# Where four one-and-two-column tiles lie in SBUF: one shared tile of 512 bytes in a two-layer transformer trunk

## The chip, the cores and the metric

The kernel runs on one core of a Trainium2 chip. The metric is the device time of one execution in microseconds (us). The profile is one execution, recorded by the hardware profiler; its span runs from the first to the last instruction.

## The reference

The kernel computes a two-layer encoder trunk on one sequence of 512 tokens and 1024 features, in float32:

```python
for i in range(DEPTH):                                   # DEPTH = 2
    h = _rmsnorm(x, norm_mix[i])
    if i % 2 == 0:                                       # layer 0
        q, k, v, u = split(h @ ab_w_in)
        a_out = diff_attention(q, k, v, ...)             # 4 heads, p1 - lambda * p2
        b_out = pool_mixer(u, pool_w, pool_scale)        # trailing means over 2, 4, 8, 16 tokens
        x = x + concat([a_out, b_out]) @ ab_w_out
    else:                                                # layer 1
        x = x + gla_mixer(h, w_in, w_gk_up, ...)         # gated linear attention, 4 heads
    h = _rmsnorm(x, norm_ffn[i])
    x = x + square(relu(h @ ffn_w1[i])) @ ffn_w2[i]      # 1024 -> 4096 -> 1024
return _rmsnorm(x, norm_final)
```

Here lambda is one number, `exp(sum(l0 * l1)) - exp(sum(l2 * l3)) + 0.2`, made of four small vectors of the input.

## The kernel before

Everything is kept transposed: features on the 128 partitions, 512 tokens along the free axis. A weight array is streamed from HBM in units of 1 MB (`load`, L92), and each half unit, 128 x 1024 float32, is split by ScalarE (`wh`, L103) and VectorE (`wl`, L104) into two parts in the type float32r. Activations are split in the same way, into a high and a low part. A product then takes three passes of TensorE (`mm3`, L123 to L127): `wh` with the high part, `wh` with the low part, `wl` with the high part. The weights are the stationary operand, a slice of 128 columns, which is 512 bytes of each partition; the activation row of 512 tokens, 2048 bytes of each partition, is the moving operand. `proj_T` (L129) makes one result of 128 features by 512 tokens from eight such triples, so 24 passes in a row, and each pass loads its own weights (LDWEIGHTS, engine PEld) while the pass before it runs.

Two kinds of rows are the moving operand of `mm3`:

- `ah` and `al` (L120): the split inputs of a block. They are read by the projections, by the output projection (`add_out`, L399) and by the first product of each feed-forward block (`ffn`, L419).
- `hi` and `lo` of L423, taken from the buffers `r16`: the split squares of the hidden layer. They are read by the second product of a feed-forward block (`ffn`, L433; `last_chunk`, L459). The profile prints every tile of `row8` and `row16` as `r`.

`ffn` handles the 4096 hidden features in four chunks of 1024. For each it makes eight rows with the first array (8 x 24 = 192 passes with `ah` and `al`), then eight results with the second array (192 passes with `r`). The two kinds of stages alternate without a pause. The last chunk of the last block is done by halves of the tokens (`last_chunk`), in 2 x 192 passes of 256 columns; each half ends in its part of the final norm and the stores of its outputs.

The gate of layer 1 has 16 passes in which the roles are mixed (L522): the moving operand is `ah` or `al`, the stationary one a tile of `row8`.

**Where tiles lie.** All tiles come from one pool. The pool gives each tag its buffers one behind the other, in the order in which the tags are first used, and rounds each tile up to a multiple of 32 bytes. Of the built program's places in a partition, in bytes:

| tag | before: start | modulo 512 | after: start | modulo 512 |
|---|---|---|---|---|
| `par`, `x`, `wraw`, `ones`, `onesr` | 16512 and on | 128 | same | 128 |
| `wh`, `wl` (4 + 4 buffers of 4096) | 51328 and on | 128 | same | 128 |
| `ah`, `al` (12 + 12 of 2048) | 84096 and on | 128 | same | 128 |
| `nacc`, `tmp`, `rb` | 133248 and on | 128 | same | 128 |
| the four small columns | 149632, 149664, 149696, 149728 | 128, 160, 192, 224 | 149632 (one tile) | 128 |
| `row8`, `row16` (8 + 16 of 2048) | 149760 and on | 256 | 150144 and on | 128 |
| `small` (24 of 32) | 198912 and on | all multiples of 32 | 199296 and on | all multiples of 32 |
| `tmp2` (6 of 2048) | 199680 and on | 0 | 200064 and on | 384 |
| `u`, `lvl`, `rb2`, `state` | 212000 and on | | all 384 bytes further | |

A buffer of `row8`, `row16`, `ah` or `al` has 2048 bytes and a slice of weights 512, so within each of these rows of the table every buffer or slice starts at the same place modulo 512.

The four small columns are the sums (L269), their exponentials (L271), minus lambda (L273) and the scaled gain (L276). A handful of instructions of a few hundred ns at most touch them, all in layer 0.

The order of the instructions on each engine is the scheduler's, and is fixed when the program is built.

Of the kernel before, what the change touches and what calls it, by code (L numbers as in the profile page):

```python
# [27 lines left out]

# columns of the packed parameter array
C_MIX0, C_FFN0, C_MIX1, C_FFN1, C_FIN = 0, 8, 16, 24, 32  # L30
# [5 lines left out]
def trunk(ctx: ExitStack, tc: tile.TileContext, xT, par, lvl, lam4, wqk0, wu0, wv0, poolw, wo0,  # L36
# [10 lines left out]

    # buffers by how long they are held: a row of 8 and a row of 16
    def row8(n=S, dt=F32):
# [17 lines left out]

    # what the tensor engine waits for goes ahead of the rest
    def soon(n=300):
        return tc.high_priority(n)  # L70

    # ---- parameters, inputs and the first unit of weights
    prm = T([P, N_PAR], "par", 1)
# [16 lines left out]

    # ---- weight streaming: raw float32 units, split into two parts of 12 bits
    def load(src):  # L92
# [14 lines left out]
    class Stream:  # L107
        """Halves of the units of one weight array, in order."""

# [19 lines left out]
    def proj_T(w, act, ts=slice(0, S)):  # L129
        """[128 features, tokens] from a half unit [128, 8, 128] and split inputs."""  # L130
        hi, lo = w
        ps = PS("mm", (P, ts.stop - ts.start))
        for kb in range(KB):
            c = slice(kb * P, (kb + 1) * P)
            ah, al = act[kb]
            mm3(ps, (hi[:, c], lo[:, c]), (ah[:, ts], al[:, ts]), kb == 0, kb == KB - 1)
        return ps

    def proj_tok(stream, act):
        """Four [128 tokens, 512 features] results from half units [128, 2, 512]."""  # L140
        pss = [PS("mm") for _ in range(NT)]
        for pair in range(KB // 2):
            wh, wl = stream.next()
            for t in range(NT):
                ts = slice(t * P, (t + 1) * P)
                for j in range(2):
                    kb = 2 * pair + j
                    c = slice(j * S, (j + 1) * S)
                    ah, al = act[kb]
                    PE.matmul(pss[t], ah[:, ts], wh[:, c], start=kb == 0, stop=False)  # L150
                    PE.matmul(pss[t], al[:, ts], wh[:, c], start=False, stop=False)  # L151
                    PE.matmul(pss[t], ah[:, ts], wl[:, c], start=False, stop=kb == KB - 1)  # L152
        return pss

    def split_scaled(src, col):
        """Parts of src * (a value per partition)."""
        ah, al = act_tiles()
        A.activation(ah, src, AF.Copy, scale=col)
        V.scalar_tensor_tensor(out=al, in0=src, scalar=col, in1=ah.bitcast(F32), op0=ALU.mult, op1=ALU.subtract)
        return ah, al  # L160
# [7 lines left out]
    def spread(r):  # L168
        """Values per token [128, n] along the free axis of every partition, in PSUM."""
        n = r.shape[-1]  # L170
        ps = PS("ax", (P, n * P))
        for t in range(n):
            PE.matmul(ps[:, t * P:(t + 1) * P], r[:, t:t + 1].to_broadcast([P, P]), ident, start=True, stop=True)
        return ps

    def col_sums(sq, c):
        """Sums over all partitions, on every partition, of a tile to which c is added."""
        n = sq.shape[-1]
        ps, hi, lo = PS("ax", (P, n)), tmp(n, F32R), tmp(n, F32R)
        A.activation(hi, sq, AF.Copy)  # L180
        V.scalar_tensor_tensor(out=lo, in0=sq, scalar=c, in1=hi.bitcast(F32), op0=ALU.add, op1=ALU.subtract)
        PE.matmul(ps, ones_r, hi, start=True, stop=False)  # L182
        PE.matmul(ps, ones_r, lo, start=False, stop=True)
        return ps
# [7 lines left out]
    def rsqrt(r, v, inv):  # L192
        """(v * inv) ** -0.5: a first value by logarithm, then one Newton step."""
        A.activation(r, v, AF.Ln, scale=inv)
        A.activation(r, r, AF.Exp, scale=-0.5)
        return newton(r, v, inv, tmp(r.shape[-1]))

    def neg_recip(r, v, inv):
        """-1 / (v * inv), in the same way."""
        t = tmp(r.shape[-1])  # L200
# [6 lines left out]
    class Norm:  # L207
        """Sums of squares over the features of x, tile by tile."""

# [24 lines left out]
    def per_token(rb):  # L234
        """One row of rb as [128 tokens, 4]."""
        ps = PS("ax", (P, NT))
# [5 lines left out]

    # ================= layer 0: attention and pooling =================
    act = []
# [17 lines left out]

    # lambda on every partition
    l4 = tmp(256)
# [3 lines left out]
    V.tensor_tensor(lp, l4v[:, :, 0, :], l4v[:, :, 1, :], ALU.mult)  # L268
    ls = T([P, 2], "lsum", 1)  # L269
    V.tensor_reduce(out=ls, in_=lp, op=ALU.add, axis=AX.X)  # L270
    le = T([P, 2], "lexp", 1)  # L271
    A.activation(le, ls, AF.Exp)
    neglam = T([P, 1], "nlam", 1)  # L273
    V.tensor_tensor(neglam, le[:, 1:2], le[:, 0:1], ALU.subtract)
    V.tensor_scalar(out=neglam, in0=neglam, scalar1=-LAM_INIT, scalar2=None, op0=ALU.add)
    sub8 = T([P, 1], "sub8", 1)  # L276
    V.tensor_scalar(out=sub8, in0=prm[:, C_SUB:C_SUB + 1], scalar1=1.0 - LAM_INIT, scalar2=None, op0=ALU.mult)
# [12 lines left out]
    def scores(h, qts):  # L290
        """Score blocks of 128 queries each, masked, in two banks; minus their scaled maxima."""
        banks = [PS("ax"), PS("ax")]
# [18 lines left out]
    def softmax(h, qt, views, neg):  # L311
        """p1 - lambda * p2, transposed, into the head's tiles."""
        n = (qt + 1) * P
# [29 lines left out]
    def attend(h):  # L343
        """The products with the values, normalised."""
        po = PS("ax")
# [26 lines left out]

    # pooling branch
    pw = tmp2().rearrange("p (g c) -> p g c", g=4)
# [24 lines left out]
    def add_out(arr, src, col):  # L399
        """x += (split inputs) @ weights; the next block's inputs and norm."""  # L400
        st = Stream(arr)
# [50 lines left out]
    def last_chunk(s2, a, rb2):  # L452
        """The end of the last block by halves of the tokens, each with its final norm."""
        for half in range(2):
# [34 lines left out]

    # constants of layer 1  # L490
    lv = T([P, NLEV + 1, P], "lvl", 1, U8)
# [10 lines left out]

    # ================= layer 1: gated linear attention =================
    with soon(800):
        smask = row8()
        G.memset(smask, 1.0)
        G.memset(smask.rearrange("p (c t) -> p c t", t=P)[:, :, 0:1], 0.0)
        # gate weights: both parts of the 16 columns side by side, so two passes make all the products;
        # four copies of them, for the stacked product of the up-projection
        gk2 = [row8(dt=F32R).rearrange("p (k a b) -> p k a b", k=4, a=4) for _ in range(2)]  # L510
        for i in range(2):
            src = gkr[:, 4 * i:4 * i + 4, :, :]
            A.activation(gk2[i][:, :, :, 0:16], src, AF.Copy)
            V.tensor_tensor(gk2[i][:, :, :, 16:32], src, gk2[i][:, :, :, 0:16].bitcast(F32), ALU.subtract)
        # rows 0-63: the weights' high part, rows 64-95: the low part
        wu = row8(dt=F32R)
# [7 lines left out]
    rb = nrm.rb()  # L524
    # rows 0-31 and 64-95: the high part of the gate's input, rows 32-63: the low part
    gkf = tmp2()
# [37 lines left out]
    def weights(h):  # L564
        """Products within chunks, and the factors across them, of one head."""
        ps = proj_T(st.next(), act)
# [8 lines left out]
        b3 = b.rearrange("p (c t) -> p c t", t=P)  # L575
        # across chunks
        e = row16()
# [16 lines left out]
        kdt.append(kd)  # L594
        # within chunks: the diagonal, then pairs (second half, first half) of ever smaller blocks
        at = row16()
# [6 lines left out]
        for l in range(NLEV - 1):  # L603
# [12 lines left out]
            if s >= 16:  # L616
                # whole blocks, which start at partitions that a product can be put at
                for p0 in range(0, P, 2 * s):
# [7 lines left out]
            for c in range(NT):  # L626
# [3 lines left out]
                              psl.rearrange("p (c t) -> p c t", t=P))  # L630
        # neighbours, as the diagonal: the products' sums over the features
        d = tmp(S // 2)
# [23 lines left out]
    def outputs(h):  # L656
        """Transposed outputs of one head, normalised: two tiles [128 features, tokens]."""
        half, hh = divmod(h, 2)
# [34 lines left out]

    # the parts of the heads, in the order that keeps every engine supplied
    for h in range(3):
# [28 lines left out]

# ---- layout on the host
def _blocks_T(w):
    """Rows in blocks of 1024, columns in units of 256: [units, 128, 2, 8 * 128]."""
    k, n = w.shape
    w = w.reshape(k // D, KB, P, n // 256, 2, P)
    return np.ascontiguousarray(w.transpose(0, 3, 2, 4, 1, 5)).reshape(-1, P, 2, 1024)  # L730


def _blocks_tok(w):
    """Columns in blocks of 512, rows in units of 512: [units, 128, 2, 2 * 512]."""
    n = w.shape[1]
# [64 lines left out]
```

## Time and profile before

| | |
|---|---|
| time, median of 3 runs | 1136.92 us (1136.45 to 1137.26) |
| span of the profiled execution | 1135.0 us |
| its own time | not listed apart; the runs' median is 1.92 us above its span |
| TensorE (PE) busy | 1118.5 us, 99% of the span |
| weight loads (PEld) | 904.5 us, 80% |
| VectorE (DVE), ScalarE (ACT) busy | 641.5 us (57%), 468.2 us (41%) |
| granted TensorE clock, mean | 0.996 of the full 2.4 GHz |

The profile draws a matmul with a duration of about 0.4 us, since it is pipelined: the next one starts some 0.23 us later. The rate of the passes is therefore read from starts, or from the count of weight loads in a stretch, not from the durations. In the views `r` is a tile of `row8` or `row16`, and `tmp` one of `tmp` or `tmp2`.

### The profile page before, as it was taken

What the parts mean: (1) busy time and instruction counts of PE and PEld (TensorE: products, weight loads), DVE (VectorE), ACT (ScalarE), POOL (GpSimd) and SP (SyncE); (2) the same over time, 40 slices, a digit from 0 to 9 for tenths busy, and PEclk for the clock granted to TensorE, in tenths of its full rate; (3) what the DMA queues carried; (4) which work ended last, traced back from release to release, by engine and by line L of the source; (5) the groups of instructions that cost most, each with busy time, mean ns of one, the idle gap of its engine ahead of it and who ended that gap; (6) DMA issues with size and microseconds to landing.
All of it is one profiled execution on the core that took longest, in us unless ns stands there. A gap on an engine that the chain in (4) does not pass through costs nothing.

```text
span 1135.0 us, 13269 instructions
## 1 busy us (share of the span) xinstructions
PE 1118.5 (99%) x5312; PEld 904.5 (80%) x5312; DVE 641.5 (57%) x1024; ACT 468.2 (41%) x748; POOL 7.2 (1%) x26
## 2 busy tenths in 40 slices
PE   8999999999999999999999999999999999999996
PEld 6676778888888888888777788888888888888896
DVE  7757866423433455456898867555323434455485
ACT  7445544323322422334645466434323313312463
POOL 0000000000000000000000000000000000000001
PEclk9999999999999999999999999999999999999998
DMA  7221233232222323222121312232232323223252
GB/s 247 80 90 38 84 109 111 74 111 79 107 103 84 111 74 111 81 106 92 58 75 38 113 38 74 74 112 88 98 109 77 111 74 112 91 96 107 79 187 75
DMA packets 19229, 107.21 MB, mean 94 GB/s; under 512 B 2048, under 2 KB 5120, under 8 KB 7008
## 3 DMA queue, kind: packets, MB, share of 16 engines
q1 hardware_dynamic: 19024, 106.34, 26.9%
q8 instruction: 42, 0.69, 0.2%
q14 instruction: 19, 0.16, 0.0%
q10 hardware_dynamic: 144, 0.03, 0.0%
HBM read 104.26 MB, written 2.10 MB: 94 GB/s over the span
## 4 chain that ended last, share of the span: by engine, by line
PE 92%; DVE 2%; issue 2%; ACT 2%; DMA 1%; SPq 0%; POOL 0%; POOLq 0%; DVEq 0%; ACTq 0%
PE psmm L127 26%; PE psmm L126 26%; PE psmm L125 26%; PE psmm L150 2%; PE psmm L152 2%; PE psmm L151 2%; PE psax L301 1%; PE psax L628 1%; PE psax L621 1%; PE psax L347 1%; DMA wraw<-in_wqk 1%; PE psax L182 1%; PE psax L678 0%; PE psax L663 0%; PE psax L329 0%
## 5 line engine op out<-in xcount | busy, mean ns | idle before, releaser
L103 ACT ACTIVATE wh<-wraw 128x1024 fp32r<-128x1024 f32 x190 | 200.9, 1059 | 517.6 <-PE psmm L126 480.1
L104 DVE TENSOR_TENSOR wl<-wraw,wh 128x1024 fp32r<-128x1024 f32 x190 | 232.2, 1223 | 264.3 <-ACT wh L103 263.6
L125 PE MATMUL psmm<-ah,wh 128*128 128x512 f32 x864 | 339.6, 393 | 4.9 <-ACT wh L250 4.9
L126 PE MATMUL psmm<-al,wh 128*128 128x512 f32 x864 | 339.4, 393 | 0.0
L127 PE MATMUL psmm<-ah,wl 128*128 128x512 f32 x864 | 338.9, 392 | 0.0
L126 PE MATMUL psmm<-r,wh 128*128 128x512 f32 (+1 forms) x576 | 213.0, 370 | 0.1
L125 PE MATMUL psmm<-r,wh 128*128 128x512 f32 (+1 forms) x576 | 213.1, 370 | 0.0
L127 PE MATMUL psmm<-r,wl 128*128 128x512 f32 (+1 forms) x576 | 213.0, 370 | 0.0
L125 PEld LDWEIGHTS psmm<-ah,wh 128*128 128x128 f32 x864 | 162.7, 188 | 41.1 <-ACT wh L250 5.6
L126 PEld LDWEIGHTS psmm<-al,wh 128*128 128x128 f32 x864 | 162.7, 188 | 36.5 <-issue 2.1
L127 PEld LDWEIGHTS psmm<-ah,wl 128*128 128x128 f32 x864 | 162.8, 188 | 35.7 <-issue 1.6
L126 PEld LDWEIGHTS psmm<-r,wh 128*128 128x128 f32 x576 | 108.2, 188 | 20.7 <-DVE r L428 0.3
L127 PEld LDWEIGHTS psmm<-r,wl 128*128 128x128 f32 x576 | 108.2, 188 | 20.4
L125 PEld LDWEIGHTS psmm<-r,wh 128*128 128x128 f32 x576 | 108.1, 188 | 20.4
L439 DVE TENSOR_TENSOR r<-r,psmm 128x512 f32<-128x512 f32 x32 | 22.0, 687 | 88.7 <-PE psmm L127 88.7
L428 DVE TENSOR_TENSOR r<-tmp,r 128x512 fp32r<-128x512 f32 x64 | 44.3, 692 | 6.5
L427 DVE TENSOR_TENSOR tmp<-tmp 128x512 f32<-128x512 f32 x64 | 43.8, 684 | 0.0
L426 ACT ACTIVATE r<-tmp 128x512 fp32r<-128x512 f32 x64 | 40.5, 634 | 2.0
L150 PE MATMUL psmm<-wh,ah 128*128 128x512 f32 x96 | 39.1, 407 | 0.0
L151 PE MATMUL psmm<-wh,al 128*128 128x512 f32 x96 | 38.5, 401 | 0.0
L152 PE MATMUL psmm<-wl,ah 128*128 128x512 f32 x96 | 38.2, 398 | 0.0
L425 ACT ACTIVATE tmp<-psmm 128x512 f32<-128x512 f32 x64 | 36.9, 577 | 0.0
(183 smaller groups left out, 813.0 us busy)
## 6 DMA issues: line engine op xcount, KB each, us to landing
wraw<-in_w2b SPq DMA_DIRECT2D x20, 1024.0 KB, 4.8
wraw<-in_w1a SPq DMA_DIRECT2D x16, 1024.0 KB, 4.8
wraw<-in_w2a SPq DMA_DIRECT2D x16, 1024.0 KB, 4.8
wraw<-in_w1b SPq DMA_DIRECT2D x16, 1024.0 KB, 4.8
wraw<-in_wo SPq DMA_DIRECT2D x8, 1024.0 KB, 4.7
wraw<-in_wqk SPq DMA_DIRECT2D x7, 1024.0 KB, 4.9
wraw<-in_wv SPq DMA_DIRECT2D x6, 1024.0 KB, 4.7
wraw<-in_wg SPq DMA_DIRECT2D x4, 1024.0 KB, 4.9
```

The costliest lines, as they stand in the source:

```text
L103: A.activation(hi, src, AF.Copy)
L104: V.tensor_tensor(lo, src, hi.bitcast(F32), ALU.subtract)
L125: PE.matmul(ps, wh, ah, start=first, stop=False)
L126: PE.matmul(ps, wh, al, start=False, stop=False)
L127: PE.matmul(ps, wl, ah, start=False, stop=last)
L150: PE.matmul(pss[t], ah[:, ts], wh[:, c], start=kb == 0, stop=False)
L151: PE.matmul(pss[t], al[:, ts], wh[:, c], start=False, stop=False)
L152: PE.matmul(pss[t], ah[:, ts], wl[:, c], start=False, stop=kb == KB - 1)
L425: A.activation(r, ps, AF.Relu)
L426: A.activation(hi, r, AF.Square)
L427: V.tensor_tensor(q, r, r, ALU.mult)
L428: V.tensor_tensor(lo, q, hi.bitcast(F32), ALU.subtract)
```

## The change

The four tiles `lsum`, `lexp`, `nlam` and `sub8` become four slices of one tile `lcol` of 128 float32 columns (512 bytes), at columns 0, 8, 16 and 24.

```diff
-    ls = T([P, 2], "lsum", 1)
+    consts = T([P, P], "lcol", 1)
+    ls, le, neglam, sub8 = (consts[:, i:j] for i, j in ((0, 2), (8, 10), (16, 17), (24, 25)))
     V.tensor_reduce(out=ls, in_=lp, op=ALU.add, axis=AX.X)
-    le = T([P, 2], "lexp", 1)
     A.activation(le, ls, AF.Exp)
-    neglam = T([P, 1], "nlam", 1)
     V.tensor_tensor(neglam, le[:, 1:2], le[:, 0:1], ALU.subtract)
     V.tensor_scalar(out=neglam, in0=neglam, scalar1=-LAM_INIT, scalar2=None, op0=ALU.add)
-    sub8 = T([P, 1], "sub8", 1)
     V.tensor_scalar(out=sub8, in0=prm[:, C_SUB:C_SUB + 1], scalar1=1.0 - LAM_INIT, scalar2=None, op0=ALU.mult)
```

Comments and docstrings are taken out too. Before, the four tiles took 4 x 32 = 128 bytes; after, the one takes 512. All that is allocated behind them lies 384 bytes further. The two built programs have the same instructions in the same order on every engine, with the same waits for the same semaphores at the same values; addresses alone differ.

## Rows read from the trace of the kernel before

**Rows 1.** The page: busy time of each engine, the granted clock in 40 slices, and the chain that ended last by engine.

```profile
span 1135.0 us, 13269 instructions
...
PE 1118.5 (99%) x5312; PEld 904.5 (80%) x5312; DVE 641.5 (57%) x1024; ACT 468.2 (41%) x748; POOL 7.2 (1%) x26
...
PEclk9999999999999999999999999999999999999998
...
PE 92%; DVE 2%; issue 2%; ACT 2%; DMA 1%; SPq 0%; POOL 0%; POOLq 0%; DVEq 0%; ACTq 0%
```

**Rows 2.** All waits of TensorE for another engine: who waited <- for whom, us in total, times, longest.

```profile
PE psmm L125 <- ACT wh L250: 4.9, 1, 4.9
PE psax L591 <- DVE tmp L588: 1.5, 1, 1.5
PE psax L173 <- DVE sm L189: 1.2, 1, 1.2
PE psax L470 <- ACT tmp L215: 1.1, 1, 1.1
PE psax L182 <- ACT tmp L180: 0.4, 1, 0.4
PE psax L329 <- DVE tmp L322: 0.3, 1, 0.3
PE psax L329 <- ACT wh L103: 0.3, 1, 0.3
```

**Rows 3.** The feed-forward block of layer 0 by its stages: busy time (and instructions) of each engine, granted clock, DMA share, GB/s. The edges are the starts of the first pass of each stage: the rest of the first stage with `ah` and `al`, then by turns a stage with `r` and one with `ah` and `al`. The count of weight loads (PEld) is that of the passes; PE's has one more, that of the pass which is still running at the edge.

```profile
core 0: us, PE busy (x) PEld busy (x) DVE busy (x) ACT busy (x) POOL busy (x), PEclk, DMA share, GB/s
185.89:223.97 38.08, 38.08 (x169) 31.53 (x168) 18.75 (x23) 15.96 (x24) 0.00 (x0) 1.00 0.25 88
223.97:268.76 44.79, 44.79 (x193) 36.05 (x192) 11.10 (x10) 13.00 (x18) 0.00 (x0) 1.00 0.27 94
268.76:312.29 43.53, 43.53 (x193) 36.03 (x192) 18.86 (x22) 16.78 (x24) 0.00 (x0) 1.00 0.28 97
312.29:357.08 44.79, 44.79 (x193) 36.03 (x192) 15.91 (x17) 9.60 (x11) 0.00 (x0) 1.00 0.27 95
357.08:400.62 43.53, 43.53 (x193) 36.04 (x192) 19.54 (x23) 16.31 (x23) 0.00 (x0) 1.00 0.27 97
400.62:445.41 44.79, 44.79 (x193) 36.05 (x192) 25.85 (x34) 11.04 (x13) 0.63 (x2) 1.00 0.27 94
445.41:488.94 43.53, 43.53 (x193) 36.04 (x192) 20.74 (x25) 16.33 (x23) 0.00 (x0) 1.00 0.27 97
488.94:533.74 44.79, 44.79 (x193) 36.04 (x192) 28.39 (x37) 18.31 (x24) 0.00 (x0) 1.00 0.28 95
```

**Rows 4.** The same view of the feed-forward block of layer 1, in the same turns from 773.38 us on; the line from 1076.44 is the first half of the tokens of the last chunk (passes of 256 columns), that from 1103.85 most of the second half.

```profile
811.46:856.25 44.79, 44.79 (x193) 36.05 (x192) 11.10 (x10) 13.00 (x18) 0.00 (x0) 1.00 0.28 94
856.25:899.78 43.53, 43.53 (x193) 36.04 (x192) 18.85 (x22) 16.79 (x24) 0.00 (x0) 1.00 0.28 97
899.78:944.58 44.79, 44.79 (x193) 36.04 (x192) 15.90 (x17) 9.60 (x11) 0.00 (x0) 1.00 0.27 94
944.58:988.11 43.53, 43.53 (x193) 36.03 (x192) 19.54 (x23) 16.30 (x23) 0.00 (x0) 1.00 0.29 97
988.11:1032.90 44.79, 44.79 (x193) 36.05 (x192) 24.34 (x31) 9.60 (x11) 0.00 (x0) 1.00 0.26 94
1032.90:1076.44 43.53, 43.53 (x193) 36.04 (x192) 20.74 (x25) 16.31 (x23) 0.00 (x0) 1.00 0.27 97
1076.44:1099.67 23.23, 23.12 (x193) 22.86 (x192) 18.97 (x30) 15.94 (x24) 0.00 (x0) 1.00 0.50 170
...
1103.85:1123.87 20.02, 20.02 (x171) 20.02 (x170) 14.14 (x29) 9.96 (x19) 2.89 (x3) 1.00 0.27 100
```

**Rows 5.** The gate's 16 passes in order of time: start us, duration us, engine, line, operation, out<-stationary and moving operands. The first is the last pass of the stage with `r`, the last the first pass of the next projection.

```profile
533.51 0.39 PE L127 MATMUL psmm<-r,wl 128*128 128x512 f32 x1
533.74 0.40 PE L522 MATMUL psmm<-ah,r 128*128 128x512 f32 x1
533.97 0.39 PE L522 MATMUL psmm<-al,r 128*128 128x512 f32 x1
...
536.77 0.39 PE L522 MATMUL psmm<-al,r 128*128 128x512 f32 x1
537.00 0.40 PE L522 MATMUL psmm<-ah,r 128*128 128x512 f32 x1
537.23 0.47 PE L522 MATMUL psmm<-al,r 128*128 128x512 f32 x1
537.54 0.40 PE L125 MATMUL psmm<-ah,wh 128*128 128x512 f32 x1
```

**Rows 6.** The passes of 256 columns in order of time, 25 starts in a row.

```profile
1112.12 0.28 PE L125 MATMUL psmm<-r,wh 128*128 128x256 f32 x1
...
1114.97 0.28 PE L125 MATMUL psmm<-r,wh 128*128 128x256 f32 x1
```

**Rows 7.** The lines of the passes with `r` in groups by shape (busy us, mean ns of one | idle before), and the two splits of the weights.

```profile
L125 PE MATMUL psmm<-r,wh 128*128 128x512 f32 x448 | 176.9, 395 | 0.0
L125 PE MATMUL psmm<-r,wh 128*128 128x256 f32 x128 | 36.1, 283 | 0.0
L104 DVE TENSOR_TENSOR wl<-wraw,wh 128x1024 fp32r<-128x1024 f32 x190 | 232.2, 1223 | 264.3 <-ACT wh L103 263.6
L103 ACT ACTIVATE wh<-wraw 128x1024 fp32r<-128x1024 f32 x190 | 200.9, 1059 | 517.6 <-PE psmm L126 480.1 <-issue 30.5 <-PE psmm L151 3.8
```

**Rows 8.** DMA issues: KB each, us from issue to landing.

```profile
wraw<-in_w2a SPq DMA_DIRECT2D x16, 1024.0 KB, 4.8
```

## The prediction

> **What bounds the kernel now.** I read the page first: TensorE is busy 1118.5 of 1135.0 us, 92% of the chain that ended last is TensorE, and the granted clock is at its full level in all but the last slice [rows 1]. Then TensorE's own waits: they come to 9.7 us in all, half of it the first weights at the start [rows 2]. Lines L125 to L127, which do all the large products, have one wait, that at the start; L470's 1.1 us is in the last norm. So inside those blocks the time is the number of passes times the spacing of the passes, and anything that changes the spacing changes the end one for one.
>
> Next I cut the two blocks into their stages [rows 3, 4]. All stages with 512 columns have 192 weight loads, so 192 passes, the same three lines, the same weights' buffers, the same clock of 1.00. Yet every stage whose moving rows are `ah` and `al` takes 43.53 us, six out of six, and every stage whose moving rows are `r` takes 44.79 us, seven out of seven [rows 3, 4]. Per pass that is 43.53 / 192 = 226.7 ns against 44.79 / 192 = 233.3 ns, 6.56 ns or 2.9% apart. (The rest of the first stage says the same for `ah`: 38.08 / 168 = 226.7 [rows 3].)
>
> What differs between the two? Not a wait, since the engine is busy the whole stretch in both. Not the other engines' load: the stages with `r` have VectorE at 11.10 to 28.39 us and ScalarE at 9.60 to 18.31, those with `ah` 18.85 to 20.74 and 16.30 to 16.79, and the time of the stages with `r` doesn't move with that threefold range of VectorE [rows 3, 4]. Not the DMAs (0.26 to 0.29 in both). What is left is the buffer the rows lie in: `ah` and `al` start at 128 modulo 512, as the weights do, `r` at 256.
>
> A second place lets the two operands change roles. In the gate's 16 passes the moving rows are `ah` and `al`, the fast ones, and the stationary operand is a `row8` tile at 256 modulo 512. From the first start to the fifteenth are 14 spacings: (537.00 - 533.74) / 14 = 232.9 ns [rows 5]. That is the slow spacing, with moving rows that elsewhere run at 226.7. So it isn't the moving row's own place, nor the values in the squares, that makes a pass dear: it is that the two operands lie 128 bytes apart modulo 512.
>
> **A rule that speaks against this.** The rows give a spacing that depends on the buffer [rows 3 to 5]. The Trainium skill, page "SBUF — State Buffer", section "SBUF: two separate sides", says that PE, ACT and DVE's own pair of ports "never wait on anyone", and its page "TensorE: Matmul & The Clock Gate", section "Step-by-step: what each phase is for", gives TensorE two independent read ports, one for the moving operand and one for the weights; by that rule places can't matter, and the change would be worth 0. By the rows the sum is the one below. The trace has two spacings for one instruction and so doesn't agree with it, unless something else than the place sets the 6.56 ns.
>
> **The change part by part.** No instruction is added, removed or moved, and no wait; four slices of a tile have the same shapes as four tiles. So there are no new costs of work. What changes is the place of everything behind the four columns, by 384 bytes:
>
> 1. *Passes of 512 columns with `r` as moving rows.* There are 3 x 448 = 1344 [rows 7], which are the seven stages of 192. `r` goes from 256 to 256 + 384 = 640, which is 128 modulo 512, where `ah`, `al`, `wh` and `wl` are. I take the spacing to become that of `ah`: 7 x (44.79 - 43.53) = 7 x 1.26 = 8.8 us less. One point no row shows: `r` will lie at 640 modulo 2048, `ah` lies at 128 modulo 2048. But eight slices of weights follow each other at steps of 512 bytes, so `ah` is paired with slices 0, 512, 1024 and 1536 bytes away from it modulo 2048; `r` will be paired with the same four distances, and the stages with `ah` contain them all at a mean of 226.7.
> 2. *The gate's 16 passes.* The `row8` tile goes to 128 modulo 512 also: 16 x (232.9 - 226.7) = 0.1 us less.
> 3. *Passes of 256 columns with `r`*, 3 x 128 = 384 [rows 7]. Their spacing now is (1114.97 - 1112.12) / 24 = 118.8 ns [rows 6]. No row shows this shape with aligned rows. Bounds by the nearest rows: if the aligned spacing is half of the aligned 512, 226.7 / 2 = 113.4 ns, 384 x 5.4 = 2.1 us less; if on the other hand the 118.8 is a good spacing and the shift costs it the 6.56 ns, 2.5 us more. 118.8 is already well above half of either spacing (116.6 for the slow one), so something other than the place seems to set it; I take 0 and keep both ends for the range.
> 4. *Everything else that moves* (`tmp2` from 0 to 384, `u`, `state`, the small tiles): read by VectorE, ScalarE and the short float32 passes, off TensorE's queue or a small share of it. VectorE and ScalarE have 2% of the chain each [rows 1], and either would have to get slower by tens of per cent there to cost some us; I take 0.
>
> Sum: 8.8 + 0.1 = 8.9 us of the span, 1135.0 to 1126.1. The runs' median stands 1.92 us above the span and nothing in the change touches what lies around it, so 1136.92 - 8.9 = 1128.0 us.
>
> *Is anything late next?* The stages with `r` would have to run at the pace of those with `ah`. Per half unit of weights (24 passes, 5.44 us at 226.7 ns) ScalarE's split takes 1.06 and VectorE's 1.22 us [rows 7]; the fullest `r` stage has VectorE at 28.39 of what will be 43.53 us [rows 3]; a unit of weights lands in 4.8 us and lasts 48 passes, 10.9 us [rows 8]. All cover the shorter stage, and the stages with `ah` run at that pace behind the same queues today. If one of these covers were gone, it would show as a wait of L125 for `wh` or of L127 for `wl`, which neither kind of stage has now.
>
> **Rivals.**
>
> - *The place is not the cause*, and the slow spacing belongs to something else in those two code places. Then nothing changes: 1136.9. For it speaks the rule above; against it the gate, where fast moving rows run slow. 7 in 100.
> - *The absolute place matters, and 640 modulo 2048 is bad.* The stationary tile of the gate could be slow for its own place, and the rows for theirs; then the relation to the weights is a coincidence, and 640 a place of which nothing is known, since all moving rows of these lines lie at 128 or 256 modulo 2048. Priced as one more step of the same size, every `r` pass gets 6.56 ns dearer: 7 x 1.26 = 8.8 us more, 1145.7. It decides as soon as a stage with `r` takes more than 44.79 us. Against it: two different operands would each need a bad place of their own, and both are the one at 256. 4 in 100.
> - *The 256-column passes take the place effect too, in full*: 1128.0 - 2.1 = 1125.9, or 1128.0 + 2.5 = 1130.5. Faster either way. 14 in 100 for a shift of more than 1 us.
> - The forecast, within about 1 us of 1128.0: 75 in 100.
>
> **How the numbers follow.** The runs of before spread over 0.8 us and about 0.2% of the time (2.3 us) is what a measurement of this kernel can tell from no change; the forecast's 8.9 us is well clear of it. The predicted time is the likeliest case. The range takes in the two ends of the 256-column passes, 1125.9 to 1130.5, rounded to 1126.0 to 1130.5; with the forecast's 75 and most of the 14 it holds about 87 in 100, and the two rivals without a gain are left out. Chances: faster by over 0.2%: 0.89; within 0.2%: 0.07; slower: 0.04.
>
> **What would show it.** Right: the seven stages with `r` at 43.5 us each, at the same counts, so that they and the six stages with `ah` read alike; the gate's 14 spacings at 3.17 us instead of 3.26; the same waits of TensorE as before; the last half of the tokens at about 20.0 us from 1095 us on. The prediction is wrong if the stages with `r` stay at 44.79 (place not the cause), if they go above it (absolute place), if they land between the two values (the distance counts in some other measure than modulo 512), or if a wait for `wl` or for L428's rows appears in them.

## The result, and the profile after

The changed kernel takes 1128.05 us in the median of 4 runs (1127.74 to 1128.10) against 1136.95 us (1136.45 to 1137.26): a ratio of 0.9921, with a 95% interval of 0.9907 to 0.9935. The forecast was 1128.0 us.

The page of the changed kernel, which answers to [rows 1]: TensorE is busy 10.5 us less, the weight loads and the other engines as long as before to 0.4 us.

```profile
span 1126.0 us, 13269 instructions
...
PE 1108.0 (98%) x5312; PEld 904.1 (80%) x5312; DVE 641.8 (57%) x1024; ACT 468.2 (42%) x748; POOL 7.3 (1%) x26
```

The span is 9.0 us shorter, so TensorE is idle 1.5 us more, most of it at the start. Its waits are those of [rows 2] but for the first line, which has two waits now, of 5.1 and 1.0 us, for the first weights:

```profile
PE psmm L125 <- ACT wh L250: 6.1, 2, 5.1
```

The stages of the changed kernel, as in [rows 3, 4]: a stage with `r`, one with `ah` and `al`, the last stage with `r` of layer 0, the first of layer 1, then the first half of the tokens of the last chunk and most of the second.

```profile
core 0: us, PE busy (x) PEld busy (x) DVE busy (x) ACT busy (x) POOL busy (x), PEclk, DMA share, GB/s
...
224.02:267.54 43.52, 43.52 (x193) 36.04 (x192) 11.10 (x10) 12.99 (x18) 0.00 (x0) 1.00 0.28 97
267.54:311.06 43.52, 43.52 (x193) 36.04 (x192) 18.86 (x22) 16.80 (x24) 0.00 (x0) 1.00 0.28 97
485.14:528.66 43.52, 43.52 (x193) 36.04 (x192) 28.41 (x37) 18.30 (x24) 0.00 (x0) 1.00 0.28 98
806.41:849.93 43.52, 43.52 (x193) 36.05 (x192) 11.10 (x10) 12.99 (x18) 0.00 (x0) 1.00 0.27 97
1067.53:1090.93 23.40, 23.29 (x193) 23.07 (x192) 18.98 (x30) 15.94 (x24) 0.00 (x0) 1.00 0.50 167
1095.12:1115.36 20.23, 20.23 (x171) 20.23 (x170) 14.17 (x29) 9.95 (x19) 2.91 (x3) 1.00 0.27 98
```

The stages with `r` now take what those with `ah` take, 43.52 us for the same 192 loads, with the other engines' busy time unchanged to 0.02 us. The two halves of the last chunk went the other way, 23.23 to 23.40 and 20.02 to 20.23 us. Their passes in order of time, as [rows 6], 25 starts in a row:

```profile
1103.12 0.28 PE L125 MATMUL psmm<-r,wh 128*128 128x256 f32 x1
...
1106.00 0.28 PE L125 MATMUL psmm<-r,wh 128*128 128x256 f32 x1
```

(1106.00 - 1103.12) / 24 = 120.0 ns, against 118.8 before. The gate's passes, as [rows 5] (the code is two lines shorter, so L520 was L522):

```profile
528.66 0.39 PE L520 MATMUL psmm<-ah,r 128*128 128x512 f32 x1
...
531.83 0.39 PE L520 MATMUL psmm<-ah,r 128*128 128x512 f32 x1
532.13 0.50 PE L520 MATMUL psmm<-al,r 128*128 128x512 f32 x1
532.47 0.40 PE L125 MATMUL psmm<-ah,wh 128*128 128x512 f32 x1
```

14 spacings now take 3.17 us instead of 3.26, as forecast, but the last pass starts 0.30 us behind its forerunner and the next projection 0.34 us behind that. From the first pass of the gate to that projection it is 3.81 us, and it was 537.54 - 533.74 = 3.80 us: the 0.1 us was given back at the stage's end.

The account of the spans, 1135.0 to 1126.0: seven stages with `r`, 7 x (44.79 - 43.52) = 8.9 us; the stages with `ah`, 43.53 to 43.52, at most 0.1 us; the gate 0; the last chunk -0.4 us; and the stretch behind the last stage, 11.1 us before and 10.6 after, +0.5 us. This last one is no effect of the change: with the same stages the next kernel below had 11.1 us there again. It is the granted clock under the last four passes of the program (L173), here before and after:

```profile
1127.27:1128.46 1.19, 1.19 (x4) 0.89 (x4) 0.00 (x0) 0.00 (x0) 0.00 (x0) 0.50 0.00 0
1118.75:1119.43 0.68, 0.68 (x4) 0.49 (x4) 0.00 (x0) 0.00 (x0) 0.00 (x0) 1.00 0.00 0
```

At 0.50, the level of 1.2 GHz, they take 0.51 us longer than at 1.00. In both kernels TensorE was busy for only 1.1 us of the 3.1 us or so behind the last large product. In the next kernel below the four passes took 1.19 us again, and in a second trace of the changed kernel 0.68 us.

### The profile page after: what moved, and what is told of

It reads as the page before. It is cut to its first block, busy times and chain, and to the rows that moved or that the text cites. A ratio compares the mean times of both kernels' runs of the same rounds, so it can differ in the third digit from the quotient of the medians.

```text
span 1126.0 us, 13269 instructions
## 1 busy us (share of the span) xinstructions
PE 1108.0 (98%) x5312; PEld 904.1 (80%) x5312; DVE 641.8 (57%) x1024; ACT 468.2 (42%) x748; POOL 7.3 (1%) x26
## 2 busy tenths in 40 slices
DMA packets 19229, 107.21 MB, mean 95 GB/s; under 512 B 2048, under 2 KB 5120, under 8 KB 7008
## 4 chain that ended last, share of the span: by engine, by line
issue 63%; PE 34%; ACT 1%; DVE 1%; DMA 0%; POOL 0%; SPq 0%; POOLq 0%; DVEq 0%
PE psmm L127 10%; PE psmm L126 9%; PE psmm L125 9%; PE psax L299 1%; PE psax L345 1%; PE psmm L150 1%; PE psmm L151 1%; PE psmm L152 1%; DMA x<-in_xT 0%; PE psax L327 0%; ACT ah L158 0%; PE psax L394 0%; ACT tmp L215 0%; POOL x L481 0%; PE psax L182 0%
## 5 line engine op out<-in xcount | busy, mean ns | idle before, releaser
L126 PE MATMUL psmm<-r,wh 128*128 128x512 f32 (+1 forms) x576 | 210.5, 366 | 0.1
L125 PE MATMUL psmm<-r,wh 128*128 128x512 f32 (+1 forms) x576 | 210.6, 366 | 0.0
L127 PE MATMUL psmm<-r,wl 128*128 128x512 f32 (+1 forms) x576 | 210.4, 365 | 0.0
```

Source lines behind the costliest of these rows:

```text
L125: PE.matmul(ps, wh, ah, start=first, stop=False)
L126: PE.matmul(ps, wh, al, start=False, stop=False)
L127: PE.matmul(ps, wl, ah, start=False, stop=last)
```

## Experiments

Two theories stood. *Relation*: a pass costs more when its moving row and its weights lie at different places modulo some number. *Absolute place*: 256 modulo 512 is bad by itself. Below, "distance" is the start of `r` less that of the weights, modulo 512 unless said otherwise.

**The shift without the shared tile.** The four columns stay four tiles; the first is wider.

```diff
-    ls = T([P, 2], "lsum", 1)
+    ls = T([P, 104], "lsum", 1)[:, 0:2]
```

> The four columns stay four tiles; the first of them is widened to 416 bytes, so that the rows behind lie where the change puts them (128 modulo 512). Theory (distance of the two operands modulo 512): the seven stages with r take 43.52 us each, as in the changed kernel, time about 1128.0 us. Rival (sharing one tile, not the shift, makes the gain): the stages stay at 44.79 us, 1136.9 us.

Measured: 1128.05 us, ratio 0.9921 (0.9893 to 0.9950). The first stage with `r`:

```profile
223.94:267.46 43.52, 43.52 (x193) 36.05 (x192) 11.10 (x10) 12.99 (x18) 0.00 (x0) 1.00 0.28 97
```

Sharing a tile has no part in it. The shift is the whole gain.

**All rows and weights at the place that was slow.** As above, and 128 bytes more ahead of the weights:

```diff
-    ones_r = T([P, P], "onesr", 1, F32R)
+    ones_r = T([P, P + 32], "onesr", 1, F32R)[:, 0:P]
```

> As the run with the columns apart, and 128 bytes more ahead of the weights' buffers, so that wh, wl, ah, al, row8 and row16 all lie at 256 modulo 512, the place that was slow before. Theory (distance): nothing changes against the changed kernel, all stages of 192 passes at 43.52 us, about 1128 us. Rival (absolute place, 256 is bad): every stage is slow, those with ah and al too, 192 passes in 44.79 us, and the kernel takes about 1128 + 2600 x 6.56 ns = 1145 us.

Measured: 1128.81 us, ratio 0.9929 (0.9907 to 0.9952). A stage with `r` and one with `ah`, all operands at 256 modulo 512:

```profile
224.13:267.65 43.52, 43.52 (x193) 36.07 (x192) 11.10 (x10) 13.00 (x18) 0.00 (x0) 1.00 0.28 97
267.65:311.17 43.52, 43.52 (x193) 36.06 (x192) 18.86 (x22) 16.81 (x24) 0.00 (x0) 1.00 0.29 97
```

At the place where the rows were slow before, the same rows are fast as soon as the weights lie there too. The absolute place has fallen as the cause.

**The low weights alone 128 bytes off.** The small columns' tiles are put ahead of and behind the buffers of `wl`:

```diff
     def w_tiles(n=1024):
-        return T([P, n], "wh", 4, F32R), T([P, n], "wl", 4, F32R)
+        hi = T([P, n], "wh", 4, F32R)
+        if not cols:
+            cols.append(T([P, 32], "lcol", 1))
+        lo = T([P, n], "wl", 4, F32R)
+        if len(cols) < 2:
+            cols.append(T([P, 96], "lcol2", 1))
+        return hi, lo
...
```

> wl alone lies at 256 modulo 512; wh, ah, al and r lie at 128 (the small columns fill the gaps ahead of and behind wl). Theory (a pass is slowed by the load of the next pass's weights that runs beside it): the pass with the low part (L126), beside which wl is loaded, gets dearer, in the stages with r and with ah alike, L125 and L127 stay at about 226.7 ns. Rival (a pass's own weights count): L127 gets dearer and L126 stays. Either way a third of the passes, 20 to 44 us per 192 by a third of 1.27: each stage about 43.9 to 44.0 us, kernel about 1132 us. Rival (absolute place of the moving rows): all as in the changed kernel, 1128 us.

Measured: 1143.67 us, 1.0061 (1.0038 to 1.0084) of the kernel before. A stage with `r` and one with `ah`:

```profile
226.13:270.50 44.37, 44.37 (x193) 36.32 (x192) 11.09 (x10) 12.99 (x18) 0.00 (x0) 1.00 0.28 95
270.50:314.88 44.37, 44.37 (x193) 36.33 (x192) 18.86 (x22) 16.79 (x24) 0.00 (x0) 1.00 0.28 95
```

Both sizes and both mechanisms missed. From start to start, the passes with `r` (448 of each line) take 226.7 ns in the first line of `mm3`, 232.5 in the second and 234.2 in the third: not one of three is dear but two, the one beside which `wl` is loaded and the one which uses it. So neither "the load beside it" nor "its own weights" is enough by itself. Since `wl` lies off `wh` here as well as off the rows, this run can't tell which of the two counts. It makes 44.37 us a stage instead of 43.9 to 44.0, and as every product with `ah` outside the two blocks pays as well, which the expected time left out, 1143.7 instead of 1132 us. What it does show: `ah` rows, fast in every other run, get dear when weights move and they don't. So the values in the rows are not the cause.

**Other distances.** One edit each, the width of the first column's tile: 112 columns for a distance of 32, 120 for 64, 24 for 192, 40 for 256, 72 for 384, 88 for 448. They were expected, in the order in which they ran:

> The first column's tile is widened so that the rows lie 64 bytes behind the weights modulo 512 (192), half of the distance before. Theory that any distance but 0 costs the same: stages with r at 44.79 us, 1136.9 us. Theory that the cost grows with the distance: between 43.52 and 44.79, about 44.2 us each, 1132.5 us.

> Rows 32 bytes behind the weights modulo 512. At 0 the stages with r take 43.52 us, at 64 they took 43.96, at 128 44.79. Theory that the cost grows with the distance: between 43.52 and 43.96, about 43.7 us (227.6 ns), time about 1129.5 us. Rival that only exact equality is cheap: 43.96 or more, 1131.9 us.

> Rows 256 bytes from the weights modulo 512, the farthest there is. Theory that the cost grows with the distance up to the middle: above 44.79 us per stage with r, 45 to 46.5 us, 1138 to 1149 us. Rival that the cost has a peak near 128 and falls again: below 44.79 us, under 1136.9 us.

> Rows 384 bytes behind the weights modulo 512, which is 128 bytes ahead of them. Theory that the distance counts in either direction alike: 44.79 us per stage with r, 1136.9 us. Rival that the direction counts (the moving row ahead of or behind the weights): another value, above or below by over 0.2 us per stage, 1135.5 us or less, or 1138.3 or more.

> Rows 448 bytes behind the weights modulo 512, 64 bytes ahead of them. Either direction alike: 43.96 us per stage with r, 1131.9 us, as at 64. Direction counts: another value by over 0.2 us per stage.

> Rows 192 bytes behind the weights modulo 512. Theory (the distance counts modulo 256): as at 448, stages with r at 44.80 us, passes of 256 columns at 113.9 ns, 1134.8 us. Rival (modulo 512): some other value; by symmetry with 320 nothing is known of it.

Measured, a stage with `r` of 192 passes of 512 columns and, behind it, 168 passes of 256 columns of the second half of the tokens, in each kernel's own trace (170 loads in the lines of the second half, since one load of the passes ahead and one of those behind fall into them). Distance 32:

```profile
224.38:269.19 44.80, 44.80 (x193) 36.00 (x192) 11.10 (x10) 13.01 (x18) 0.00 (x0) 1.00 0.28 94
1104.18:1123.87 19.69, 19.69 (x171) 19.69 (x170) 14.11 (x29) 9.95 (x19) 2.91 (x3) 1.00 0.28 101
```

Distance 64:

```profile
225.12:269.09 43.96, 43.96 (x193) 36.06 (x192) 11.10 (x10) 13.00 (x18) 0.00 (x0) 1.00 0.28 96
1099.41:1119.29 19.87, 19.87 (x171) 19.87 (x170) 14.13 (x29) 9.95 (x19) 2.92 (x3) 1.00 0.28 99
```

Distance 192:

```profile
224.49:269.29 44.80, 44.80 (x193) 35.92 (x192) 11.10 (x10) 12.99 (x18) 0.00 (x0) 1.00 0.28 94
1103.63:1122.78 19.14, 19.14 (x171) 19.14 (x170) 14.00 (x29) 9.96 (x19) 2.91 (x3) 1.00 0.28 104
```

Distance 256:

```profile
223.63:267.15 43.52, 43.52 (x193) 36.05 (x192) 11.10 (x10) 12.99 (x18) 0.00 (x0) 1.00 0.28 97
1094.65:1114.89 20.23, 20.23 (x171) 20.23 (x170) 14.18 (x29) 9.95 (x19) 2.91 (x3) 1.00 0.27 99
```

Distance 384:

```profile
223.93:268.72 44.79, 44.79 (x193) 36.04 (x192) 11.11 (x10) 13.00 (x18) 0.00 (x0) 1.00 0.27 94
1103.81:1123.82 20.02, 20.02 (x171) 20.02 (x170) 14.16 (x29) 9.96 (x19) 2.90 (x3) 1.00 0.27 99
```

Distance 448:

```profile
223.96:268.76 44.80, 44.80 (x193) 35.91 (x192) 11.10 (x10) 13.01 (x18) 0.00 (x0) 1.00 0.27 94
1102.98:1122.12 19.14, 19.14 (x171) 19.14 (x170) 14.00 (x29) 9.96 (x19) 2.91 (x3) 1.00 0.28 103
```

Put together by the distance modulo 256 (times are single runs but for the distances 0 and 128; the passes of 512 columns are the stage over 192):

| distance modulo 256 | seen at | stage with `r`, us | ns per pass | 168 passes of 256 columns, us | time, us |
|---|---|---|---|---|---|
| 0 | 0, 256 | 43.52, 43.52 | 226.7 | 20.23, 20.23 | 1128.05, 1127.56 |
| 32 | 32 | 44.80 | 233.3 | 19.69 | 1136.83 |
| 64 | 64 | 43.96 | 229.0 | 19.87 | 1131.91 |
| 128 | 128 (before), 384 | 44.79, 44.79 | 233.3 | 20.02, 20.02 | 1136.95, 1136.95 |
| 192 | 192, 448 | 44.80, 44.80 | 233.3 | 19.14, 19.14 | 1135.42, 1134.80 |

Three pairs of kernels that differ by 256 bytes agree in the stages to 0.01 us, and the third pair was forecast. So the period is 256, not 512. "The cost grows with the distance" fell twice: 32 is dearer than 64, and 256, the farthest, is as good as 0. The direction counts as well: 64 costs 0.4 us a stage and 192, which is 64 the other way, 1.3 us. (That 384 reads like 128 is no sign against it, since modulo 256 the two are one distance.) For passes of 256 columns the order is another one: 0 is the dearest and 192 the cheapest.

**Every second row off.** The buffers of `row16` are 2176 bytes apart, so that they lie on and off by turns (the first column's tile has 40 columns, as for the distance 256, and 5 buffers of `state` instead of 6 make room):

```diff
-        return T([P, n], "r16", 16, dt)
+        return T([P, S + 32], "r16", 16, dt)[:, 0:n]
...
```

> The buffers of row16 are 2176 bytes apart in place of 2048, so that every second one lies 128 bytes off the weights modulo 256 and every second one on them (5 buffers of state in place of 6 make room). In layer 0 the buffers fall so that in the first and third stage with r the high rows are on and the low rows off (one pass of three off, L126), and in the second and fourth the high rows off and the low rows on (L125 and L127 off). Theory that each pass pays for the place of its own moving row: first and third stage 43.52 + 64 x 6.6 ns = 43.9 us, with L126 alone dear; second and fourth 44.4 us, with L126 at about 226.7 ns. Rival that a pass off its place also delays the next one, as the passes beside the shifted low weights suggest: first and third 44.4 us, second and fourth 44.8 us, with no pass at 226.7 ns behind a dear one.

Measured: 1132.02 us, in one run. The first stage with `r` (low rows off), the one with `ah` behind it, and the second with `r` (high rows off):

```profile
223.94:267.89 43.95, 43.95 (x193) 35.99 (x192) 11.10 (x10) 13.00 (x18) 0.00 (x0) 1.00 0.27 96
267.89:311.41 43.52, 43.52 (x193) 36.04 (x192) 18.86 (x22) 16.79 (x24) 0.00 (x0) 1.00 0.28 97
311.41:355.35 43.95, 43.95 (x193) 36.01 (x192) 15.91 (x17) 9.61 (x11) 0.00 (x0) 1.00 0.28 97
```

From start to start, in the first stage: 226.7, 234.0 and 226.0 ns for the three lines, so the pass with its row off pays 7.3 ns and its neighbours nothing. That was the theory's number; the rival, in which the next pass is late too, had 44.4 us. In the second stage: 232.2, 226.1 and 228.4 ns; again those that are off pay, but two of them together only as much as the one before (43.95 us, expected 44.4). In layer 1, where the buffers happened to fall in mixed order, the stages took 44.32 to 44.37 us, and passes whose own row was on its place took up to 236 ns. So there is no fixed price per pass that is off; what the other passes near it do counts too.

**A version with the best distance for each shape.** Distance 0 modulo 256 for the stages of 512 columns, and for the last chunk the weights 64 bytes further in their buffers, which makes the distance 192 (the first column's tile has 40 columns and `state` 5 buffers, as in the kernel above):

```diff
     def w_tiles(n=1024):
-        return T([P, n], "wh", 4, F32R), T([P, n], "wl", 4, F32R)
+        c = slice(shift[0], shift[0] + n)
+        return T([P, n + 64], "wh", 4, F32R)[:, c], T([P, n + 64], "wl", 4, F32R)[:, c]
...
             if c == 3 and col is None:
+                shift[0] = 16
                 return last_chunk(s2, a, rb2)
...
```

> Built from what the runs showed: the rows of row16 lie 0 modulo 256 from the weights for the passes of 512 columns, and for the last chunk (passes of 256 columns) the weights are written 64 bytes further into their buffers, so that the rows lie 192 modulo 256 from them, where passes of 256 columns took 113.9 ns against 120.0. The weights' buffers are 4352 bytes apart, so that they lie at 128 and at 384 modulo 512 by turns; the state has 5 buffers in place of 6 to make room. Theory (distance modulo 256): stages of 192 passes of 512 columns at 43.52 us throughout, the last chunk 384 x 6 ns = 2.3 us shorter than in the changed kernel, about 1125.5 us. Rival (distance modulo 512): half of the weights' buffers are off, about 1128 us or more; since 256 measured as 0, its spacings can't tell here, but a mixed order of buffers could. Rival (weights at a place of their own cost something): the last chunk isn't shorter, 1127.8 us.

> The changed kernel beside the one above, on the same chip and in the same rounds: 1128.0 us, 0.992 of the kernel before.

Measured in the same rounds: 1126.34 us (1125.90 to 1127.95), ratio 0.9906 (0.9892 to 0.9920), and the changed kernel 1128.25 us (1127.93 to 1128.85), ratio 0.9925 (0.9912 to 0.9938). The intervals overlap; the medians are 1.9 us apart, less than the 0.2% that can be told. So it isn't shown to be faster than the changed kernel. The trace is of the longest of its five runs, 1127.95 us (the other four took 1125.90 to 1126.37). It shows the part that was meant, in the line from 1095.80, 19.14 us instead of 20.23:

```profile
225.06:268.58 43.52, 43.52 (x193) 36.05 (x192) 11.10 (x10) 13.00 (x18) 0.00 (x0) 1.00 0.28 97
1068.56:1091.67 23.11, 22.95 (x193) 22.68 (x192) 18.96 (x30) 15.95 (x24) 0.00 (x0) 1.00 0.49 169
1095.80:1114.94 19.14, 19.14 (x171) 19.14 (x170) 14.00 (x29) 9.97 (x19) 2.90 (x3) 1.00 0.29 104
```

Together these stretches of the last chunk are 1.4 us shorter than in the changed kernel, where 2.3 us were expected of the whole. The first half took 23.11 us, where the kernels at distances 192 and 448 had 22.50 and 22.51: the passes here ran at spacings of 117 to 119 ns through most of that half and at 113 to 114 in the second; why the first half didn't come down is open. In this kernel half of the weights' buffers lie 256 bytes off the other half, and the stages of 512 columns still take 43.52 us, a second sign of the period of 256.

## Why the prediction was right, point by point

- *The passes' spacing sets the time of the blocks.* Right: the seven stages became 8.9 us shorter, and the span 9.0 us.
- *It is the place of the two operands to each other.* Right, and shown by the run with everything at 256: a slow place became fast when the weights went there.
- *"Modulo 512".* Too wide. The rows of before had only distances 0 and 128, which can't tell 256 from 512. The change itself is unhurt, since 0 is 0 either way, but 128 bytes more or 128 bytes less in the small tiles would have done as well as 384.
- *640 modulo 2048 is as good as 128.* Right, 43.52 against 43.52 us.
- *The gate, 0.1 us less.* The spacing came out as forecast (3.17 us for 14), the saving did not, since the next projection began no earlier.
- *Passes of 256 columns, taken as 0 between -2.1 and +2.5 us.* They cost 0.4 us more: 120.0 ns for 118.8. The reason given for the 0, that something other than the place seems to set them, fell: places alone moved the 168 passes between 19.14 and 20.23 us. That the good place for one shape is the dearest of those measured for the other wasn't foreseen, and that the 0 came so near is luck: for these 168 passes the distances 128 and 0 happen to be 0.2 us apart.
- *Nothing else is late.* Right for the two blocks: the engines' busy times are those of before, and no new wait appears in them. The second wait for the first weights, 1.0 us at 10.42 us, isn't the change's cost: the kernel at distance 256 has one wait of 4.9 us there, as before, and nothing of it is left where the first stage with `r` begins, at 224.02 us instead of 223.97.
- *The sum, 1128.0 for 1128.05 us.* So close a hit is luck in part. In the traces the last chunk took 0.4 us more than forecast and the gate gave nothing back, and the 0.5 us of the clock at the very end made up for both.
- *VectorE's "threefold range" over the stages with `r`.* 11.10 to 28.39 us is a factor of 2.6; the argument holds with it.
- *The rule of the read ports.* The Trainium skill's sentence in "SBUF — State Buffer", section "SBUF: two separate sides", that PE never waits on anyone would have made the change worth nothing, as the prediction read it. That reading fell: places alone moved the kernel between 1127.6 and 1143.7 us. Whether the ports meet, or something else makes the places count, no run here shows.

What stays open is why the places count. A load beside a pass, the pass's own weights, and what the passes near it did all showed up (the runs with the low weights off and with every second row off), and no single one of them explains all the spacings.

## What to carry to other kernels

When the same instruction runs at two spacings in two stages with the engine always busy, compare where the operands lie before looking for waits: counts of weight loads between stage starts show 3% that no wait shows. For float32r passes of 512 columns with a weight load each, start the moving rows and the weights at the same place modulo 256 bytes, which was the best of the distances measured in this kernel (0.8% of its time against 128); small tiles allocated in between shift everything behind them, so pad them to a multiple of 256. Measure other shapes apart: passes of 256 columns wanted another distance.

## What the runs showed of the hardware that was not expected

- At distance 0 modulo 256 a pass of 512 columns takes 226.67 ns (43.52 us / 192) and one of 256 columns 120.0 ns, at a granted clock of 1.00: 512 / 2.4 + 13.3 and 256 / 2.4 + 13.3, the same 13.3 ns on top. The Trainium skill's page "TensorE: Matmul & The Clock Gate", section "Wait — 56ns, not 53.3ns?", gives N / 2.4 GHz + about 2.5 ns, 215.7 ns measured at 512. No stage of these passes, each with a weight load of its own, came down to that.
- At some other distances the spacing is no longer even. In the kernel before, from start to start, it went by turns between 229 and 237.5 ns; at 192 and 448 it is even again, every pass at 233 or 234.
- Passes of 256 columns went below 120.0 ns at every distance but 0, down to 113.9 ns (19.14 us / 168) at 192. So the 13.3 ns are no floor for them.
- The chain that ended last reads "PE 92%" before and "issue 63%; PE 34%" after, though TensorE is busy 43.52 of 43.52 us in the stages. This is no sign of the change: a second trace of the same changed kernel reads "PE 92%", and the kernel at distance 384, with the times of before, "issue 63%; PE 34%". The chain's view can name the same time either way from trace to trace, and the windows are the view to read.
